# Compressed attention of a hybrid decoder layer: the softmax transposed per head pair to 96 rows, and its product with the values as one fp32r matmul of 512 columns

## The chip, the cores and the metric

The kernel runs on one core of a Trainium2 chip. The metric is the device time of one execution in microseconds; lower is better. A core has five engines that run side by side, each with its own in-order instruction queue: TensorE (PE in the rows; its weight loads are PEld), VectorE (DVE), ScalarE (ACT), GpSimd (POOL), and SyncE (SP), which here issues the transfers. TensorE writes into PSUM, a small memory of eight banks of 128 partitions by 512 float32 values; ScalarE and VectorE carry results from there to SBUF, the working memory.

## The reference

Two layers run one after the other on 256 tokens of width 1024. Each computes three attention branches from the same normalised input and merges them. The change touches one part of the first branch, the compressed attention: 256 tokens are compressed to 15 blocks for each of 2 key groups, and the 8 query heads (4 for each group) attend to the blocks of their group.

```python
def block(args):                       # one block of 128 queries
    qb, i = args
    t = i * Q_BLOCK + jnp.arange(Q_BLOCK)
    s = jnp.einsum('bqgrd,bngd->bgrqn', qb, k_c) * scale        # n: 15 compressed blocks
    p_c = _masked_softmax(s, cmp_end[None, :] <= t[:, None])
    o_c = jnp.einsum('bgrqn,bngd->bqgrd', p_c.astype(v_c.dtype), v_c)
...
o = g[..., 0, :] * to_bthd(o_c) + g[..., 1, :] * to_bthd(o_s) + g[..., 2, :] * to_bthd(o_w)
```

The other two terms, the selected blocks and the sliding window, and the two other branches are unchanged, as are the projections around them.

## The kernel before

Almost all the work is matrix products with weights that are streamed from HBM in chunks of 256 rows by up to 512 columns (`load_w`). A product of full accuracy is made of three products in the one-pass type fp32r: ScalarE rounds each chunk to a high half `whi` (line 161), VectorE forms the remainder `wlo` (line 162), and `gemm_steps` (line 263) adds high by high, low by high and high by low into the banks `mm`. The chunks are split two ahead of their use (`LEAD`), with three buffers for each half. `silu_path_T` (line 824) is the same with the operands' roles exchanged.

The attention is cut into units that are woven into these products. Each call of `tick` lets the unit in front compute its scores (`scores`), the one before it transpose its softmax (`transpose`), and the one before that multiply it with the values (`product`). The small matmuls of these steps stand in a list, `small`, and `hand_out` spreads them over the next chunk's matmuls, each tied behind one of them with `issue_after`. Within such ties the framework orders each engine's instructions itself, by a simulated timeline (`schedule_with_timeline_sim=True`), so the order in a trace is not that of the program.

The compressed attention is the class `Cmp`: one unit for each block of 128 queries and each layer, so four in all. In each layer the unit of the first block comes before the window units of the second block, and that of the second block before the forgetting branch. `Cmp.softmax` leaves in `e` (tile `ce`) 128 queries by 8 heads by 16 columns, the 15 probabilities and a zero. `Cmp.transpose` turns all of it in one 128 by 128 transposition (`put_T`, line 217) into a bank `T`, and `evac` copies it to `eT`, in turns on ScalarE (line 338) and VectorE (line 340). `Cmp.product` (line 979) multiplies it, in plain float32, with `Vc`: four products of 128 columns, one for each pair of heads, into the one bank `O`; a plain float32 product appears as two matmuls in the trace. Then `done_c` (lines 991 to 994) adds the result to the other two terms and splits it for the branch's projection.

`value` makes `Vc` once a layer: a product of the compressed hidden rows with `w2` (line 900) and one VectorE instruction (line 901) that writes the 128 by 512 block matrix with the mask `bmask`. `split_evac` (lines 371 and 373) is the usual way out of a transposition for the other units: a rounded copy by ScalarE into `PTh`, then the remainder by VectorE into `PTl`, two buffers each.

Of the kernel before, what the change touches and what calls it, by code (L numbers as in the profile page):

```python
# [31 lines left out]
def shape_constants():  # L32
    half = 32
    inv = (10000.0 ** (-np.arange(half, dtype=np.float32) / np.float32(half))).astype(np.float32)
    ang = np.arange(T, dtype=np.float32)[:, None] * inv[None, :]
    cos, sin = np.cos(ang).astype(np.float32), np.sin(ang).astype(np.float32)
    cos2 = np.concatenate([cos, cos], 1).reshape(NT, 128, 64).transpose(1, 0, 2)
    sin2 = np.concatenate([-sin, sin], 1).reshape(NT, 128, 64).transpose(1, 0, 2)
    ident = np.eye(128, dtype=np.float32)
    p = np.arange(128)  # L40
    ntri = -(p[:, None] <= p[None, :]).astype(np.float32)
    even = (p[:, None] == 2 * np.arange(64)[None, :]).astype(np.float32)
    odd = (p[:, None] == 2 * np.arange(64)[None, :] + 1).astype(np.float32)
    t = np.arange(T).reshape(NT, 128).T
    n = np.arange(15)
    cmask = np.where(16 * n[None, None, :] + 31 <= t[:, :, None], 0.0, NEG).astype(np.float32)

    bmask = 0.5 * (p[:, None] // 16 == np.arange(8)[None, :]).astype(np.float32)
    cm = np.where(p[None, :] <= p[:, None], 0.0, NEG).astype(np.float32)
    parts = [ident, cos2, sin2, ntri, even, odd, cmask, bmask, cm]  # L50
    cst = np.concatenate([a.reshape(128, -1) for a in parts], 1).astype(np.float32)
    return np.ascontiguousarray(cst)
# [7 lines left out]
def hybrid_kernel(ctx: ExitStack, tc, I, cst_d, out_d):  # L60
# [249 lines left out]
    def take(n):  # L310
        off[0] += n
        return cst[:, off[0] - n:off[0]]
# [4 lines left out]
    ntri = take(128)  # L317
    sel = [take(64), take(64)]
    cmask = take(30).rearrange("p (t n) -> p t n", t=2)
    bmask = take(8)  # L320
    cm = take(128)
    mhalf = S([128, 16], "mhalf")
    nc.gpsimd.memset(mhalf, -0.5)
# [247 lines left out]
    for l in range(2):  # L571
# [266 lines left out]
            mark((nm, l))  # L838


        Vc = S([128, 512], "Vc").rearrange("p (r g d) -> p r g d", r=4, g=2)

        def compress_out(i, hp):
            ch = S([128, 128], "cmph")
            nc.scalar.activation(ch, hp[:, 0:128], AF.Copy)

            def s1():
                q = pT()
                nc.tensor.transpose(q[:, 0:128], ch, ident)
                hs = S([128, 30], "cmphs")  # L850
                for g in range(2):
                    nc.vector.tensor_reduce(hs[:, g * 15:g * 15 + 15],
                                            q[:, 0:128].rearrange("p (j g n) -> p g n j", j=4, g=2)[:, g, 0:15],
                                            axis=AXX, op=ALU.add)
                th = S([128, 30], "cmpth")
                nc.scalar.activation(th, hs, AF.Tanh, scale=0.5)

                def s2():
                    if i == 0:
                        sT = S([128, 30], "sT")  # L860
                        nc.vector.scalar_tensor_tensor(sT, th, 1.0, hs, op0=ALU.add, op1=ALU.mult)
                        later(1, lambda: key(sT))
                    else:
                        sT = S([128, 4, 2, 16], "sTv")
                        nc.gpsimd.memset(sT, 0.0)
                        nc.vector.scalar_tensor_tensor(hs, th, 1.0, hs, op0=ALU.add, op1=ALU.mult)
                        nc.vector.tensor_copy(sT[:, :, :, 0:15], heads(hs, 2)[:, None].to_broadcast([128, 4, 2, 15]))
                        later(1, lambda: value(sT))
                later(1, s2)

            def key(sT):
                kp = pT()
                nc.tensor.matmul(kp[0:30, 0:64], sT, w2[:, 0, :], start=True, stop=True)
                kk = S([30, 64], "ckk")
                nc.vector.tensor_scalar(kk, kp[0:30, 0:64], 0.5, None, op0=ALU.mult)
                sq, ss, r = SQ()[0:30, 0:64], S([30, 1], "css"), S([30, 1], "cr")
                nc.scalar.activation(sq, kk, AF.Square, accum_out=ss)
                nc.gpsimd.tensor_scalar(r, ss, 1.0 / 64, EPS, op0=ALU.mult, op1=ALU.add)
                nc.gpsimd.tensor_tensor(r, r, mhalf[0:30, 0:1], op=ALU.pow)

                def s4():
                    kn = S([128, 128], "cmph")[0:30].rearrange("p (g d) -> p g d", g=2)
                    for g in range(2):
                        nc.vector.scalar_tensor_tensor(kn[:, g, :], kk, r, g4[0:30, 1, :], op0=ALU.mult, op1=ALU.mult)

                    def s5():
                        q2 = pT()
                        nc.tensor.transpose(q2[:, 0:30], kn.rearrange("p g d -> p (g d)"), ident[0:30, 0:30])
                        nc.scalar.activation(kcT[0][:, :, 0:15], heads(q2[:, 0:30], 2), AF.Copy)
                        for g in range(2):  # L890
                            gs = slice(g * 64, (g + 1) * 64)
                            nc.vector.tensor_tensor(kcT[1][gs, g, 0:15], q2[gs, g * 15:g * 15 + 15],
                                                    kcT[0][gs, g, 0:15].bitcast(F32), op=ALU.subtract)
                        mark(("kc", l))
                    later(1, s5)
                later(1, s4)

            def value(sT):
                vp = pT()
                nc.tensor.matmul(vp[:, 0:64], sT.rearrange("p r g n -> p (r g n)"), w2[:, 1, :], start=True, stop=True)  # L900
                nc.vector.tensor_tensor(Vc.rearrange("p r g d -> p (r g) d"), vp[:, 0:64][:, None, :].to_broadcast([128, 8, 64]), b3(bmask, 8, 64),
                                        op=ALU.mult)
                mark(("vc", l))
            later(1, s1)

# [19 lines left out]
        class Cmp:  # L925
# [40 lines left out]

            def transpose(self):
                def out(q):
                    self.eT = S([128, 128], "eT")
                    evac(self.eT, q[:, 0:128])  # L970
                put_T([lambda: self.e.rearrange("p h n -> p (h n)")], out)

            def product(self):
                box = []

                def one(r):
                    if not box:
                        box.append(pO())
                    nc.tensor.matmul(box[0][:, r * 128:(r + 1) * 128], Vc[:, r].rearrange("p g d -> p (g d)"), self.eT,  # L979
                                     start=True, stop=True)  # L980
                for r in range(4):
                    put(lambda r=r: one(r), *([lambda: self.done(box[0])] if r == 3 else []))

        oa_ = act_pair(4, "oT")

# [272 lines left out]
```

## Time and profile before

| | us |
|---|---|
| median of 3 runs | 637.11 (636.88 to 637.46) |
| the profiled execution | 637.58 |
| its span | 635.9 |

The profile is of one execution, of which the span covers all but 1.7 us. It gives busy time of each engine, waits and what ended them, the chain of work that ended last, and every instruction in order of time. A matmul's shown duration contains the time that it spends in the pipeline: matmuls that follow each other overlap, so what one costs TensorE is read from the distance of starts, or from the chain, where pieces do not overlap.

### The profile page before, as it was taken

Reading aid. Unit: us, or ns where it says so; the run is one execution under the profiler, and the core shown is the slowest. Engines: PE = TensorE matmul, PEld = TensorE weight load, DVE = VectorE, ACT = ScalarE, POOL = GpSimd, SP = SyncE. Lnnn points to the kernel's source line nnn. Section 1 sums busy time; section 2 is a strip of 40 time slices with the busy share of each in tenths; the row PEclk is TensorE's granted clock in tenths of the full one; section 3 lists DMA queues with packets and bytes.
Section 4 is the critical chain, followed back from the end, with each engine's and each line's share of the span. In section 5 each row is a group of like instructions: output and inputs, shape, how many; then the busy total and the mean of one; then the engine's idle time right before and its main releaser. Section 6 shows DMA issues by size and latency. Waiting matters only on the chain.

```text
span 635.9 us, 10280 instructions
## 1 busy us (share of the span) xinstructions
PE 623.9 (98%) x3567; PEld 532.2 (84%) x3567; DVE 472.7 (74%) x841; ACT 381.7 (60%) x810; POOL 175.5 (28%) x234
## 2 busy tenths in 40 slices
PE   7999999999999999999999999999999999999997
PEld 5699997788998888888887989977889888888885
DVE  3678897668977976956576799965799678777563
ACT  5766667455756676544476666855476666664441
POOL 1813403343413220704012233140053051042130
PEclk8999999999999999999999999999999999999999
DMA  8759775375345454546754695544644365445442
GB/s 298 170 159 282 230 173 161 101 207 169 104 130 139 132 161 133 164 138 195 234 178 109 195 336 159 150 140 133 172 122 140 99 172 160 137 128 166 166 149 82
DMA packets 75412, 104.51 MB, mean 164 GB/s; under 512 B 16832, under 2 KB 31456, under 8 KB 75360
## 3 DMA queue, kind: packets, MB, share of 16 engines
q1 hardware_dynamic: 75296, 103.84, 55.6%
q8 instruction: 28, 0.46, 0.3%
q14 instruction: 24, 0.20, 0.1%
q10 hardware_dynamic: 64, 0.02, 0.0%
HBM read 102.78 MB, written 1.05 MB: 163 GB/s over the span
## 4 chain that ended last, share of the span: by engine, by line
PE 94%; ACT 2%; DMA 1%; DVE 1%; issue 1%; SPq 0%; ACTq 0%
PE mm L263 60%; PE mm L824 11%; PE S L263 6%; PE T L217 6%; PE O L482 4%; PE S L1011 2%; DMA wraw<-in_w_mem_kv_dram 1%; PE S L1110 1%; PE S L918 1%; PE S L1170 1%; PE S L1108 1%; PE O L979 1%; ACT whi L161 1%; PE S L938 1%; ACT sq L363 0%
## 5 line engine op out<-in xcount | busy, mean ns | idle before, releaser
L162 DVE TENSOR_TENSOR wlo<-wraw,whi 128x1024 fp32r<-128x1024 f32 (+3 forms) x177 | 220.5, 1249 | 95.3 <-ACT whi L161 93.1
L161 ACT ACTIVATE whi<-wraw 128x1024 fp32r<-128x1024 f32 (+3 forms) x177 | 183.8, 1039 | 113.0 <-PE mm L263 71.4
L263 PE MATMUL mm<-whi,aTl 128*128 128x512 f32 (+1 forms) x480 | 189.2, 394 | 0.7 <-DVE aTl L396 0.6
L263 PE MATMUL mm<-whi,aTh 128*128 128x512 f32 (+1 forms) x480 | 188.0, 397 | 1.2 <-ACT whi L161 1.1
L263 PE MATMUL mm<-wlo,aTh 128*128 128x512 f32 (+1 forms) x480 | 184.7, 395 | 1.0 <-DVE wlo L162 1.0
L537 POOL TENSOR_TENSOR P<-P,d 128x512 f32<-128x512 f32 (+1 forms) x64 | 61.2, 971 | 208.0 <-DVE d L533 99.3
L263 PEld LDWEIGHTS mm<-whi,aTh 128*128 128x128 f32 x480 | 90.1, 189 | 19.6 <-ACT whi L161 2.3
L263 PEld LDWEIGHTS mm<-wlo,aTh 128*128 128x128 f32 x480 | 90.6, 189 | 18.3 <-DVE wlo L162 1.9
L263 PEld LDWEIGHTS mm<-whi,aTl 128*128 128x128 f32 x480 | 90.6, 189 | 17.4 <-DVE aTl L396 1.5
L824 PE MATMUL mm<-aTh,wlo 128*128 128x256 f32 x192 | 54.9, 288 | 0.0
L824 PE MATMUL mm<-aTl,whi 128*128 128x256 f32 x192 | 54.8, 286 | 0.0
L824 PE MATMUL mm<-aTh,whi 128*128 128x256 f32 x192 | 54.6, 285 | 0.0
L526 ACT ACTIVATE P<-S,m 128x256 f32<-128x256 f32 (+1 forms) x112 | 46.7, 427 | 7.6 <-DVE m L523 6.5
L1084 POOL TENSOR_TENSOR big<-big,t 128x512 f32<-128x512 f32 x16 | 28.2, 1776 | 58.9 <-DVE t L1083 53.9
L371 ACT ACTIVATE PTh<-T 128x512 fp32r<-128x512 f32 (+1 forms) x48 | 26.9, 560 | 25.7 <-PE T L217 25.4
L263 PE MATMUL mm<-whi,oTh 128*128 128x512 f32 x96 | 38.5, 404 | 0.6 <-ACT PTh L371 0.6
L263 PE MATMUL mm<-wlo,oTh 128*128 128x512 f32 x96 | 38.8, 407 | 0.0
L263 PE MATMUL mm<-whi,oTl 128*128 128x512 f32 x96 | 38.7, 403 | 0.0
L824 PEld LDWEIGHTS mm<-aTh,wlo 128*128 128x128 f32 x192 | 36.6, 191 | 0.4
L824 PEld LDWEIGHTS mm<-aTh,whi 128*128 128x128 f32 x192 | 36.6, 191 | 0.3
L824 PEld LDWEIGHTS mm<-aTl,whi 128*128 128x128 f32 x192 | 36.6, 191 | 0.2
L523 DVE TENSOR_REDUCE m<-S 128x2 f32<-128x512 f32 (+3 forms) x64 | 32.3, 515 | 2.7 <-PE S L1170 2.5
(229 smaller groups left out, 1002.9 us busy)
## 6 DMA issues: line engine op xcount, KB each, us to landing
wraw<-in_w_in_dram SPq DMA_DIRECT2D x112, 512.0 KB, 3.8
wraw<-in_w_out_dram SPq DMA_DIRECT2D x16, 512.0 KB, 4.1
wraw<-in_w_mem_kv_dram SPq DMA_DIRECT2D x15, 512.0 KB, 4.4
wraw<-in_w_branch_a_dram SPq DMA_DIRECT2D x16, 256.0 KB, 4.0
wraw<-in_w_branch_b_dram SPq DMA_DIRECT2D x8, 512.0 KB, 3.6
wraw<-in_w_branch_m_dram SPq DMA_DIRECT2D x8, 512.0 KB, 3.6
wraw<-in_w_in_dram SPq DMA_DIRECT2D x8, 408.0 KB, 3.6
wraw<-in_w_in_dram SPq DMA_DIRECT2D x8, 384.0 KB, 3.5
```

The lines of the kernel that those rows point to most:

```text
L161: nc.scalar.activation(wh[:, j, :n], v[:, j, :n], AF.Copy)
L162: nc.vector.tensor_tensor(wl[:, j, :n], v[:, j, :n], wh[:, j, :n].bitcast(F32), op=ALU.subtract)
L217: nc.tensor.transpose(q[0][0:b.shape[1], i * 128:(i + 1) * 128], b, ident)
L263: mi = nc.tensor.matmul(o_, a[:, kg, ts], w_[:, k, :n], start=(kg == 0 and i == 0), stop=(last and k == 1 and i == 2))
L371: nc.scalar.activation(hi, src, AF.Copy, scale=scale)
L482: nc.tensor.matmul(self.O[0:lhsT.shape[1], cols], lhsT, rhs, start=first, stop=False, skip_group_check=True)
L523: nc.vector.tensor_reduce(m[:, n:n + c], heads(sp[:, o_:o_ + w * c], c), axis=AXX, op=ALU.max, negate=True)
L526: nc.scalar.activation(self.P[:, k], sp[:, k], AF.Exp, bias=m[:, n:n + 1], accum_out=d[:, n:n + 1])
L537: nc.gpsimd.tensor_tensor(P3, P3, b3(d[:, n:n + c], c, w), op=ALU.mult)
L824: mi = nc.tensor.matmul(o_, w_, a[:, kg, :], start=(kg == 0 and j % 2 == 0 and i == 0), stop=(kg == 7 and i == 2), skip_group_check=True)
L1011: put(lambda j=j, k_=k_: nc.tensor.matmul(sp()[:, j * 256:(j + 1) * 256], QA[:, g, r0 + j, ts], k_, start=(j == 0 and k_ is kh), stop=(j = ...
L1084: nc.gpsimd.tensor_tensor(uv, uv, tn, op=ALU.add)
```

## The change

`Cmp.transpose` makes four transpositions instead of one, each of two heads (32 columns of `e`), into the same 32 partitions of one bank, side by side: 32 by 512. Three instructions carry it out of PSUM: a rounded copy (high part) to partitions 0 to 31, the remainder (low part) to 32 to 63, and the rounded copy again to 64 to 95. They write a tile of 96 by 512 that takes its buffers from those of `PTh`. `value` makes, in place of `Vc`, the tile `V3` of 96 by 128: the values' high part against the first two groups of rows and their low part against the third, so that `Cmp.product` is one fp32r matmul of 96 rows and 512 columns. The mask `bmask` shrinks from 8 to 2 columns, `sTv` from four copies to three.

```diff
-        Vc = S([128, 512], "Vc").rearrange("p (r g d) -> p r g d", r=4, g=2)
+        V3 = S([128, 128], "V3", dt=F32R)[0:96]
...
-                        sT = S([128, 4, 2, 16], "sTv")
+                        sT = S([128, 3, 2, 16], "sTv")
...
-                nc.tensor.matmul(vp[:, 0:64], sT.rearrange("p r g n -> p (r g n)"), w2[:, 1, :], start=True, stop=True)
-                nc.vector.tensor_tensor(Vc.rearrange("p r g d -> p (r g) d"), vp[:, 0:64][:, None, :].to_broadcast([128, 8, 64]), b3(bmask, 8, 64),
+                nc.tensor.matmul(vp[0:96, 0:64], sT.rearrange("p r g n -> p (r g n)"), w2[:, 1, :], start=True, stop=True)
+                vf = S([128, 128], "cmph")[0:96]
+                nc.vector.tensor_tensor(heads(vf, 2), vp[0:96, 0:64][:, None, :].to_broadcast([96, 2, 64]), b3(bmask[0:96], 2, 64),
                                         op=ALU.mult)
+                nc.scalar.activation(V3, vf, AF.Copy)
+                nc.vector.tensor_tensor(V3[64:96], vf[64:96], V3[64:96].bitcast(F32), op=ALU.subtract)
...
             def transpose(self):
                 def out(q):
-                    self.eT = S([128, 128], "eT")
-                    evac(self.eT, q[:, 0:128])
-                put_T([lambda: self.e.rearrange("p h n -> p (h n)")], out)
+                    self.eT = eT = S([128, 512], "PTh", bufs=2, dt=F32R)[0:96]
+                    nc.scalar.activation(eT[0:32], q[0:32], AF.Copy)
+                    nc.vector.tensor_tensor(eT[32:64], q[0:32], eT[0:32].bitcast(F32), op=ALU.subtract)
+                    nc.scalar.activation(eT[64:96], q[0:32], AF.Copy)
+                e = self.e.rearrange("p h n -> p (h n)")
+                put_T([lambda r=r: e[:, r * 32:(r + 1) * 32] for r in range(4)], out)
 
             def product(self):
-                box = []
-
-                def one(r):
-                    if not box:
-                        box.append(pO())
-                    nc.tensor.matmul(box[0][:, r * 128:(r + 1) * 128], Vc[:, r].rearrange("p g d -> p (g d)"), self.eT,
-                                     start=True, stop=True)
-                for r in range(4):
-                    put(lambda r=r: one(r), *([lambda: self.done(box[0])] if r == 3 else []))
+                def one():
+                    O = pO()
+                    nc.tensor.matmul(O, V3, self.eT, start=True, stop=True)
+                    self.done(O)
+                put(one)
```

## Rows read from the trace of the kernel before

**Rows 1.** The page of the profile: its parts 1 (busy time and share of the span, with the number of instructions) and 2 (tenths of busy time in 40 slices, and the granted clock of TensorE in tenths).

```profile
span 635.9 us, 10280 instructions
...
PE 623.9 (98%) x3567; PEld 532.2 (84%) x3567; DVE 472.7 (74%) x841; ACT 381.7 (60%) x810; POOL 175.5 (28%) x234
...
PEclk8999999999999999999999999999999999999999
```

**Rows 2.** The waits of TensorE over the whole span: who it waited for, us in total, times, longest.

```profile
PE T L217 <- DMA big<-in_mem_dram: 2.6, 1, 2.6
...
PE mm L263 <- ACT whi L161: 1.1, 3, 0.6
PE mm L263 <- DVE wlo L162: 1.0, 2, 0.5
```

**Rows 3.** The chain of waits in order of time from 150 to 165 us, around the first compressed unit of the first layer (start, us, what).

```profile
154.89 0.55 PE T L217 x5
...
156.39 1.39 PE mm L263 x6
157.77 0.89 PE O L979 x8
158.66 0.44 PE T L217 x4
```

**Rows 4.** The same view from 186 to 193 us, around the second compressed unit of the first layer.

```profile
187.41 0.11 PE T L217
187.51 0.59 PE mm L824 x5
...
191.76 0.89 PE O L979 x8
```

**Rows 5.** The same view around the two compressed units of the second layer (460 to 470 and 495 to 503 us).

```profile
467.29 0.89 PE O L979 x8
...
501.27 0.89 PE O L979 x8
```

**Rows 6.** The same view from 78 to 80 us and from 135 to 143 us: float32 products with a stationary side of 64 columns (L720) and the product that makes the compressed values (L900).

```profile
78.84 0.62 PE T L720 x16
...
136.17 0.17 PE T L900 x2
```

**Rows 7.** TensorE's instructions in order of time, 213.6 to 213.8 us (start, us, line, operands: moving and then stationary side, then the size of the stationary and of the moving side): products with moving sides of 128 columns.

```profile
213.61 0.22 PE L482 MATMUL O<-PTh,fV 128*128 128x128 f32 x1
213.67 0.22 PE L482 MATMUL O<-PTl,fV 128*64 128x128 f32 x1
213.73 0.43 PE L1108 MATMUL S<-aTl,aTh 65*128 65x128 f32 x2
```

**Rows 8.** Groups of instructions by line, with shapes kept apart (count, then busy us, mean ns of one, idle before): copies out of PSUM and the differences beside them.

```profile
L338 ACT ACTIVATE eT<-T x2: 277/277/277, 155.0 to 464.5; 128x128 f32<-128x128 f32 x2
...
L373 DVE TENSOR_TENSOR PTl<-T,PTh 128x512 fp32r<-128x512 f32 x32 | 21.8, 681 | 1.1 <-ACT PTh L371 1.1
...
L371 ACT ACTIVATE PTh<-T 128x512 fp32r<-128x512 f32 x32 | 19.0, 595 | 18.9 <-PE T L217 18.8
...
L554 ACT ACTIVATE tm<-O 64x512 f32<-64x512 f32 x8 | 4.7, 591 | 2.2 <-PE O L482 2.1
...
L901 DVE TENSOR_TENSOR Vc<-T,cst 128x512 f32<-128x512 f32 x2 | 1.4, 692 | 0.1
```

**Rows 9.** Readers of one PSUM tile on two engines: ScalarE and VectorE in order of time (lines 661 to 663), and who waited for line 794.

```profile
81.92 0.27 ACT L661 ACTIVATE KH<-T 64x128 fp32r<-64x128 f32 x1 [0.39 <-DVE KL L663]
...
81.62 0.27 DVE L663 TENSOR_TENSOR KL<-T,KH 64x128 fp32r<-64x128 f32 x1
...
  ACT big L793: 3.8, 2
```

**Rows 10.** ScalarE in order of time after the transposition of the first compressed unit.

```profile
155.04 0.28 ACT L338 ACTIVATE eT<-T 128x128 f32<-128x128 f32 x1
155.47 0.60 ACT L371 ACTIVATE PTh<-T 128x512 fp32r<-128x512 f32 x1 [0.16 <-PE T L217]
```

**Rows 11.** VectorE in order of time in the same place.

```profile
155.62 0.68 DVE L366 TENSOR_REDUCE ss<-sq 128x8 f32<-128x512 f32 x1
...
157.52 0.69 DVE L1048 TENSOR_TENSOR t<-mm,rf 128x512 f32<-128x512 f32 x1 [0.29 <-POOL rf L352]
...
163.38 3.19 DVE L162 TENSOR_TENSOR wlo<-wraw,whi 128x1024 fp32r<-128x1024 f32 x2
```

**Rows 12.** VectorE in order of time around the second compressed unit of the first layer.

```profile
187.55 0.29 DVE L340 COPY eT<-T 128x128 f32<-128x128 f32 x1 [1.49 <-PE T L217]
...
192.69 0.69 DVE L991 TENSOR_TENSOR o<-o,O 128x512 f32<-128x512 f32 x1 [1.97 <-PE O L979]
```

**Rows 13.** Busy time of the engines in stretches (us, then PE, PEld, DVE, ACT, POOL with their instructions, granted clock, DMA share, GB/s).

```profile
160.00:175.00 15.00, 15.00 (x102) 13.71 (x101) 14.85 (x28) 11.79 (x28) 5.42 (x4) 1.00 0.42 112
...
470.00:490.00 20.00, 20.00 (x145) 18.71 (x144) 19.57 (x38) 14.22 (x32) 7.83 (x6) 1.00 0.44 126
```

**Rows 14.** TensorE in order of time after the first compressed unit: a product of the window branch, and two products of a gemm.

```profile
163.33 0.28 PE L482 MATMUL O<-PTh,VN 128*128 128x256 f32 x1
...
166.56 0.39 PE L263 MATMUL mm<-whi,aTl 128*128 128x512 f32 x1
...
167.85 0.48 PE L263 MATMUL mm<-wlo,aTh 128*128 128x512 f32 x1
```

More of the change, by code (lines that the diff above doesn't have):

```diff
@@ L46, in shape_constants @@
     cmask = np.where(16 * n[None, None, :] + 31 <= t[:, :, None], 0.0, NEG).astype(np.float32)
-    bmask = 0.5 * (p[:, None] // 16 == np.arange(8)[None, :]).astype(np.float32)
+    bmask = 0.5 * ((p[:, None] // 16) % 2 == np.arange(2)[None, :]).astype(np.float32)
     cm = np.where(p[None, :] <= p[:, None], 0.0, NEG).astype(np.float32)
@@ L319, in hybrid_kernel @@
     cmask = take(30).rearrange("p (t n) -> p t n", t=2)
-    bmask = take(8)
+    bmask = take(2)
     cm = take(128)
@@ L863, in s2 @@
                     else:
-                        sT = S([128, 4, 2, 16], "sTv")
+                        sT = S([128, 3, 2, 16], "sTv")
                         nc.gpsimd.memset(sT, 0.0)
                         nc.vector.scalar_tensor_tensor(hs, th, 1.0, hs, op0=ALU.add, op1=ALU.mult)
-                        nc.vector.tensor_copy(sT[:, :, :, 0:15], heads(hs, 2)[:, None].to_broadcast([128, 4, 2, 15]))
+                        nc.vector.tensor_copy(sT[:, :, :, 0:15], heads(hs, 2)[:, None].to_broadcast([128, 3, 2, 15]))
                         later(1, lambda: value(sT))
```

## Prediction

> **What bounds the kernel now.** I read the page first: TensorE is busy 623.9 of 635.9 us, VectorE 74% and ScalarE 60%, and the granted clock is at its upper level (2.4 GHz) in every slice but the first [rows 1]. A busy TensorE can still hide stalls, so the second view is its waits: the longest is 2.6 us at the start of the kernel, for a transfer; for the high and low halves of the weights, which the two other engines make, it waits 1.1 and 1.0 us in the whole span [rows 2]. So time that is taken out of TensorE's queue is taken out of the kernel, unless a new wait eats it. Third, the chain of waits around the compressed units, four in all: it stays on TensorE from piece to piece, and there each piece has its own, not overlapping, time [rows 3 to 5].
>
> **What the product costs now, and then.** The eight matmuls of a compressed product take 0.89 us, the same in all four units [rows 3 to 5], or 0.11 each. Their moving side has only 128 columns. Six fp32r matmuls of 512 columns take 1.39 [rows 3], or 0.23 each, and two fp32r matmuls that move 128 columns with a stationary side of 64 and then 128 start 0.06 apart [rows 7]. So the short ones are not limited by the 128 columns that they move, but by the 128 that they load. The new product moves 512 columns once and its load hides behind the matmul before it: 0.23. No row has a matmul of 96 rows; the nearest, with 128, move the same columns, so I take 0.23 at both ends. Saved: 0.89 - 0.23 = 0.66 us a unit.
>
> **What the transpositions cost.** A lone transposition costs 0.11 [rows 4], a group of four 0.44 [rows 3]: again 0.11 for each 128 columns loaded. The change makes four that load 32 columns and move 128 (the identity). No row shows that shape. Upper bound: the load of 32 costs as much as that of 128, or the four are scattered, each in front of a matmul that loads 128; then 0.44. Lower bound: sixteen small products that load 64 and move 64 columns take 0.62 [rows 6], 0.039 each; three of these and 0.11 for the last, behind which a full load has to follow, are 0.23. Between: three that move 128 columns at 0.06 [rows 7], and 0.11, make 0.29. I take this, since the step of 0.06 comes from the row with the same moving side and a short load. Against today's 0.11 the transpositions add 0.18 (0.12 to 0.33).
>
> The Trainium skill has a rule for this ("TensorE: Matmul & The Clock Gate", section "LDWEIGHTS (loading the stationary operand)"): a load takes its number of columns divided by 1.2, in ns, whatever the number of rows. For 128 columns that is 107 ns, which the 0.11 of rows 3 bears out; for 64 it would be 53 ns, more than the 0.039 us of rows 6. By the rule, with the 56 ns that the same page gives for 128 moving columns, a group would be an estimated 0.275 us, and the four units together would save 0.06 us more than by my rows.
>
> **The sum on TensorE.** A unit gains 0.66 - 0.18 = 0.48 us (0.33 to 0.54); four units 1.92 (1.3 to 2.2). The product of `value`, two matmuls at 0.17 once a layer [rows 6], loads 96 columns in place of 128: a quarter of at most 0.11 for one load that isn't hidden, 0.03 in each layer, so 0.03 for both as a middle between 0 and 0.06. Together -1.95 us. On the profiled execution (span 635.9, its own time 637.58) that gives 635.6. The median of the runs shown is 0.47 below that execution; on it the sum gives **635.2**, with 634.8 to 635.8 from the bounds.
>
> **What is added on the two other engines.** In place of one copy of 128x128 (0.28 on ScalarE in the first units, 0.29 on VectorE in the second [rows 8, 12]) there are two ScalarE copies and one VectorE difference of 32x512. A copy of 64x512 takes 591 ns and one of 128x512 595 [rows 8], so the number of partitions doesn't matter, and I take 0.60 and 0.68 for 32 too. ScalarE gets 0.92 us more in a first unit and 1.20 in a second; VectorE 0.68 and 0.39. In `value`, VectorE's 692 ns [rows 8] give way to 96x128 and 32x128, by the nearest rows about 0.29 and 0.27 [rows 9, 12]; ScalarE gets 0.28. It is done long before the product, and I cost it at nothing.
>
> I cost the rest at nothing too: what hides it is TensorE's other work, the gemm's chunks that are split two ahead. If that cover were gone, VectorE's additions would be worth 2 x 0.68 + 2 x 0.39 = 2.1 us, and ScalarE's 4.2. VectorE is the engine to look at: it is busy 14.85 of 15 us right after the first unit, and 19.57 of 20 at the same place of the second layer [rows 13]. The gap before L1048 there is 0.29 us [rows 11], so 0.4 of the new 0.68 pushes its whole queue back, up to the two weight halves at 163.38 [rows 11]. Around the second units it idles for 1.49 and 1.97 us [rows 12].
>
> **The added wait.** Before, one instruction carried `eT` out. Now there are three that read one bank, and the rows say how such readers go: in lines 661 to 663 ScalarE begins its next copy only when VectorE has ended its read of the same tile (81.62 + 0.27, then 81.92), and L793 has waited 3.8 us for L794 [rows 9]. So the second copy, though it needs nothing from the difference, waits for it: 0.60 + 0.68 + 0.60 = 1.88 us in a row. The Trainium skill names a reason ("PSUM — Partial Sum Buffer", section "Terms"): two engines on one bank and the same partitions at once are an error, so that they must be kept apart; the trace agrees, as rows 9 show. Behind the waiting copy stand, in ScalarE's queue, the rounded copy at 155.47 [rows 10] and the exponentials that follow it. Their users come late: the product that reads that copy starts at 163.33 [rows 14].
>
> Does TensorE wait for the chain? The first copy can start at 155.04 [rows 10], and the product stood at 157.77 [rows 3]: 2.7 us. Four transpositions end 0.18 later, which leaves some 2.5 for 1.88, and 0.6 for what stands in the way: L366 in VectorE's queue (0.68 from 155.62, [rows 11]) and the other copy on ScalarE (0.60 [rows 10]). Tight, but the order isn't fixed: after 166.56 TensorE went on past a weight half that came late, and took it up at 167.85 [rows 14]. For the second units there are 4.2 us (187.51 to 191.76 [rows 4]). The buffers don't add a wait: `eT` joins the two of `PTh`, the unit before has been multiplied by then, and the next unit to need its buffer has the product in front of it already.
>
> **The rivals.**
> - *Half of it is given back in the first units.* If the chain meets L366 and the copy at 155.47, it is about 0.7 over; or VectorE's push of 0.4 reaches the weight halves. At 0.4 to 0.7 in each of the two first units, 0.8 to 1.4 of the 1.95 are lost: 636.0 to 636.6 on the median, 636.3 in the middle. For it: rows 11 and 13. Against it: TensorE itself runs 0.48 earlier, and it found other work at 166.56.
> - *The small transpositions are not cheaper.* At the upper bound of 0.44 a group the gain is 4 x 0.33 = 1.3: 635.8. For it: no row shows 32 columns, and `hand_out` may scatter them. Against it: rows 6.
> - *The product stands and waits.* This one ends slower. TensorE's queue is in order; if the product keeps its place while its operand comes through two busy queues, with a pair of weight halves like that of rows 11 (3.19 us) ahead of the difference, beside which only the first copy's 0.60 runs, the chain becomes 1.88 + 3.19 - 0.60 = 4.5, 2.0 over the 2.5 there are. Two first units then cost 4.0, and the sum is +2.05: 639.2. It decides the sign by over 0.2% from a chain of some 4.1 us. Against it: no weight half stands between 155 and 157.5 in rows 10 and 11.
>
> **How the numbers follow.** Forecast 0.58, half given back 0.20, transpositions not cheaper 0.11, product waits 0.11. The likeliest is the forecast: 635.2. A measurement tells about 0.2% from no change, 1.27 us here; below 635.84 is faster. The forecast lies there but for its edge, the second rival by half; the first is within 0.2%. That makes faster 0.60, same 0.29, slower 0.11. The range runs from 634.5 (the lower bounds, and 0.3 for the reordering of other work) to 636.8 (the first rival's end with 0.2 on top); it leaves the third rival out and some of each edge.
>
> **What the next profile would show.** Right: in the chain, one L-product of 0.23 in place of 0.89 in each unit, groups of four transpositions near 0.29, TensorE busy about 2 us less and its waits as short as before. The first rival: TensorE idle before L482, L263 or the new product, ended by VectorE, some 0.5 each at 155 to 170 and 465 to 480. The second: groups of 0.44. The third: idle of over 1.5 us before the new product, ended by ScalarE. What would make me wrong altogether: a 96-row matmul of 512 columns that takes two passes, or a new order that leaves waits elsewhere.

## The result, and the profile after

The change makes the kernel slower: 645.21 us (median of 6 runs, 642.16 to 645.78) against 637.32 of the kernel before (6 runs, 636.88 to 638.2), a ratio of 1.0116 [1.0105, 1.0128]. The forecast was 635.2, its range 634.5 to 636.8. The profiled execution took 645.2, 7.6 more than that of before.

The page of the kernel after, for [rows 1]:

```profile
span 643.5 us, 10246 instructions
...
PE 627.4 (97%) x3551; PEld 533.6 (83%) x3551; DVE 474.2 (74%) x845; ACT 385.8 (60%) x818; POOL 176.3 (27%) x234
...
PEclk9999999999998999999999999999999899999999
```

The span is 7.6 us longer. TensorE is busy 3.5 us more, though it has less to do, and idle 4.1 us more (643.5 - 627.4 = 16.1, before 635.9 - 623.9 = 12.0). The line of the granted clock has two new 8s, and its first slice is no 8 any more. So two things are to be found: idle time, and time at a lower clock.

What the prediction had costed comes first: the chain of waits around the first compressed unit, for [rows 3].

```profile
154.77 0.88 PE T L217 x8
...
155.89 0.47 PE S L1014 x4
...
159.36 0.23 PE O L983
159.60 0.44 PE T L217 x4
```

The product costs 0.23, as forecast. The transpositions don't cost 0.29: eight of them, the unit's four of 32 columns and a window unit's four of 128, take 0.88, which is 0.11 each and 0.44 for the four. TensorE's queue shows the two groups starting at 154.61 and 155.05. Their weight loads did become shorter (the loads of `ce` in the kernel before and then in this one: how many, then the least, median and most ns):

```profile
L217 PEld LDWEIGHTS T<-cst,ce x4: 137/138/141, 154.5 to 496.6; 128*128 128x128 f32 x4
...
L217 PEld LDWEIGHTS T<-cst,ce x16: 94/95/96, 154.4 to 502.7; 128*32 128x32 f32 x16
```

The three instructions out of PSUM in the same place, on ScalarE and then on VectorE, in order of time, for [rows 10, 11]:

```profile
155.25 0.59 ACT L974 ACTIVATE PTh<-T 32x512 fp32r<-32x512 f32 x1 [0.44 <-PE T L217]
...
157.24 0.59 ACT L976 ACTIVATE PTh<-T 32x512 fp32r<-32x512 f32 x1
```

```profile
156.22 0.68 DVE L975 TENSOR_TENSOR PTh<-T,PTh 32x512 fp32r<-32x512 f32 x1
...
159.58 0.69 DVE L1051 TENSOR_TENSOR t<-mm,rf 128x512 f32<-128x512 f32 x1 [0.36 <-POOL rf L352]
160.18 0.15 DVE L533 TENSOR_TENSOR d<-d,gat 128x2 f32<-128x2 f32 x1
```

The three come one after the other, as forecast (155.25, 156.22, 157.24), and the product, at 159.36, doesn't wait for them; it has moved 1.6 back, behind other work (before, 157.77). Around this unit TensorE doesn't wait at all, as the prediction said. But two lines lower VectorE's queue stands in a new order: L1051 (before: L1048), which waits for GpSimd, is ahead of L533; before, L533 came first, at 158.78. This small step of a window unit is 1.40 us later, and GpSimd's work on that unit (L537) starts at 160.50, before at 159.61.

TensorE's waits over the whole span, for [rows 2]:

```profile
PE S L1111 <- ACT P L526: 4.7, 2, 2.3
```

This line is new: 4.7 us, in two waits, one in each layer. Most of the others stand in the first 32 us, where nothing was changed. Here is the place in the first layer, before and after. First the kernel before, TensorE and then VectorE in order of time:

```profile
193.88 1.03 PE L1110 MATMUL S<-aTl,aTh 65*128 65x256 f32 x4
194.88 0.50 PE L263 MATMUL mm<-whi,aTh 128*128 128x512 f32 x1
```

```profile
193.41 0.69 DVE L993 SCALAR_TENSOR_TENSOR o<-o,sg 128x512 f32<-128x512 f32 x1
194.14 0.69 DVE L808 SCALAR_TENSOR_TENSOR sg<-sq,mm 128x512 f32<-128x512 f32 x1
```

Then the kernel after, TensorE and VectorE:

```profile
193.61 0.49 PE L983 MATMUL O<-PTh,V 96*128 96x512 f32 x1
196.44 0.49 PE L1111 MATMUL S<-aTl,aTh 65*128 65x128 f32 x2 [2.34 <-ACT P L526]
...
197.34 0.50 PE L263 MATMUL mm<-whi,aTh 128*128 128x512 f32 x1
...
197.99 0.63 PE L263 MATMUL mm<-wlo,aTh 128*128 128x512 f32 x1
198.42 0.63 PE L263 MATMUL mm<-whi,aTh 128*128 128x512 f32 x1
...
201.31 0.39 PE L263 MATMUL mm<-whi,aTl 128*128 128x512 f32 x1
201.54 0.40 PE L263 MATMUL mm<-wlo,aTh 128*128 128x512 f32 x1
```

```profile
194.27 0.29 DVE L523 TENSOR_REDUCE m<-S 128x1 f32<-128x128 f32 x1
194.48 0.68 DVE L994 TENSOR_TENSOR o<-o,O 128x512 f32<-128x512 f32 x1
195.08 0.62 DVE L523 TENSOR_REDUCE m<-S 128x1 f32<-128x128 f32 x2
195.61 0.68 DVE L996 SCALAR_TENSOR_TENSOR o<-o,sg 128x512 f32<-128x512 f32 x1
...
196.61 0.67 DVE L808 SCALAR_TENSOR_TENSOR sg<-sq,mm 128x512 f32<-128x512 f32 x1
```

Line 808 is the last step of a SiLU gate: it writes a buffer of `sg`, and it is the last reader of one of the three banks `mm`. Lines 993 (before) and 996 (after) close the second compressed unit, and are the last readers of the buffer of `sg` that this L808 is to write. In the kernel before, L993 starts at 193.41, L808 at 194.14, and the gemm at L263 goes on at 194.88, without idle time but right behind it: the slack is zero. In the kernel after, the product is at 193.61 (before 191.60), L994 at 194.48, L996 at 195.61 and L808 at 196.61. TensorE stands 2.34 us behind the product. Between the closing steps stand row maxima of the next units (L523), so VectorE's queue makes the step longer still. Two things come back to TensorE late: at 196.44 a bank `S` for the next scores, given back by the exponentials (L526), which had waited for VectorE's row maxima behind L994; and at 197.34 the bank `mm`, given back by L808, with which the gemm goes on. The profile names the first, since it came first; that the second is the one to look at is shown only by the experiments below.

And look at the distance of the starts after the stall. From 197.99 on they are 0.43 apart, where 0.23 is the rule; from 201.31 they are 0.23 again. That is the granted clock. The stretches table shows it in both layers (columns as in [rows 13]):

```profile
198.00:201.40 3.40, 3.40 (x11) 2.80 (x10) 2.22 (x7) 0.61 (x1) 0.97 (x2) 0.53 0.00 0
508.00:510.00 2.00, 1.36 (x4) 1.16 (x5) 2.00 (x5) 2.00 (x8) 0.97 (x2) 0.60 0.00 0
510.00:517.00 7.00, 7.00 (x26) 5.67 (x24) 3.62 (x8) 2.22 (x4) 0.97 (x2) 0.63 0.00 0
```

A clock of 0.53 for 3.4 us loses 1.6, 0.60 for 2 us 0.8, and 0.63 for 7 us 2.6: 5 us, an estimate from these three lines. With it the 7.6 is nearly accounted for. Busy: about +5 for the clock, -1.3 for the work that the change saves (four units of 0.33, see below), together near the measured +3.5. Idle: +4.7 for the two stalls, and what is left to the measured +4.1, -0.6, for all other waits together.

### The profile page after: what moved, and what is told of

The parts are those of the page before. It is cut to its first block, busy times and chain, and to the rows that moved or that the text cites. A ratio compares the mean times of both kernels' runs of the same rounds, so it can differ in the third digit from the quotient of the medians.

```text
span 643.5 us, 10246 instructions
## 1 busy us (share of the span) xinstructions
PE 627.4 (97%) x3551; PEld 533.6 (83%) x3551; DVE 474.2 (74%) x845; ACT 385.8 (60%) x818; POOL 176.3 (27%) x234
## 4 chain that ended last, share of the span: by engine, by line
PE 94%; DVE 2%; ACT 2%; DMA 1%; issue 0%; SPq 0%; ACTq 0%; DVEq 0%
PE mm L263 61%; PE mm L824 11%; PE T L217 6%; PE S L263 6%; PE O L482 4%; PE S L1014 2%; DMA wraw<-in_w_mem_kv_dram 1%; PE S L1113 1%; PE S L922 1%; PE S L1173 1%; DVE wlo L162 1%; PE S L1111 1%; ACT whi L161 1%; ACT sq L363 1%; PE S L942 0%; DVE S L517 0%
## 5 line engine op out<-in xcount | busy, mean ns | idle before, releaser
L263 PE MATMUL mm<-whi,aTl 128*128 128x512 f32 (+1 forms) x480 | 190.7, 397 | 0.8 <-DVE aTl L396 0.6
L263 PE MATMUL mm<-whi,aTh 128*128 128x512 f32 (+1 forms) x480 | 188.6, 399 | 1.8 <-ACT aTh L395 1.2
L263 PE MATMUL mm<-wlo,aTh 128*128 128x512 f32 (+1 forms) x480 | 184.9, 396 | 1.1 <-DVE wlo L162 1.1
L537 POOL TENSOR_TENSOR P<-P,d 128x512 f32<-128x512 f32 (+1 forms) x64 | 59.9, 949 | 203.2 <-DVE d L533 102.8
L263 PEld LDWEIGHTS mm<-whi,aTh 128*128 128x128 f32 x480 | 91.1, 190 | 19.8 <-ACT aTh L395 1.6
L263 PEld LDWEIGHTS mm<-wlo,aTh 128*128 128x128 f32 x480 | 91.1, 190 | 19.0 <-DVE wlo L162 1.9
L263 PEld LDWEIGHTS mm<-whi,aTl 128*128 128x128 f32 x480 | 91.2, 190 | 18.1 <-DVE aTl L396 1.4
L526 ACT ACTIVATE P<-S,m 128x256 f32<-128x256 f32 (+1 forms) x112 | 47.0, 430 | 13.3 <-DVE m L523 12.2
L371 ACT ACTIVATE PTh<-T 128x512 fp32r<-128x512 f32 (+1 forms) x48 | 26.9, 559 | 26.9 <-PE T L217 24.6
L263 PE MATMUL mm<-whi,oTh 128*128 128x512 f32 x96 | 38.8, 404 | 0.4 <-DVE t L1137 0.4
L263 PE MATMUL mm<-whi,oTl 128*128 128x512 f32 x96 | 38.6, 402 | 0.0
L263 PE MATMUL mm<-wlo,oTh 128*128 128x512 f32 x96 | 38.5, 406 | 0.0
L373 DVE TENSOR_TENSOR PTl<-T,PTh 128x512 fp32r<-128x512 f32 (+1 forms) x48 | 30.7, 640 | 5.7 <-ACT PTh L371 5.4
```

Source lines behind the costliest of these rows:

```text
L263: mi = nc.tensor.matmul(o_, a[:, kg, ts], w_[:, k, :n], start=(kg == 0 and i == 0), stop=(last and k == 1 and i == 2))
L371: nc.scalar.activation(hi, src, AF.Copy, scale=scale)
L373: nc.vector.tensor_tensor(lo, src, hi.bitcast(F32), op=ALU.subtract)
L526: nc.scalar.activation(self.P[:, k], sp[:, k], AF.Exp, bias=m[:, n:n + 1], accum_out=d[:, n:n + 1])
L537: nc.gpsimd.tensor_tensor(P3, P3, b3(d[:, n:n + c], c, w), op=ALU.mult)
```

## The experiments

Theory 1: TensorE starves at the end of the second compressed unit of each layer, through a ring of buffers. `sg` has two buffers for the three gates SA, SB and SM. The gate of SM takes SA's buffer, and SA's last reader is the second compressed unit's closing step. So a later end of this unit holds L808; L808 holds a bank of `mm`; and the bank holds the second half of the next gemm, the memory branch's query projection. In the kernel after, a fall of the clock follows each stall. The rivals look where the prediction had looked: the serial way out itself, with ScalarE's second copy held behind VectorE; the work added to VectorE and ScalarE; the price of the product or of the transpositions. Each expectation says what its theories give. In the code shown, `...` stands for lines left out.

**The gate's buffer freed.** SM's gate gets the buffer of a tile that is idle at that time (`Lc`), in the kernel after (e1) and in that of before (e2):

```diff
...
-            sg = S([128, 4, T], "sg", bufs=2)
+            sg = S([128, 4, T], "Lc") if nm == "SM" else S([128, 4, T], "sg", bufs=2)
...
```

> The changed kernel, with one thing more: the third SiLU gate of a layer (SM) is written to the buffer of Lc, which is idle by then, and no longer waits for the first gate's buffer, whose last reader is the end of the second compressed unit (L996). Theory 1 (starvation): TensorE ran dry at 193.8 to 196.4 us and at the same place of layer 2 because the gate's VectorE step (L808), and behind it the bank that the next gemm half needs, stood behind the compressed unit's end; the two stalls of 2.3 us and the fall of the clock to 1.2 GHz after them (3.4 and 6.8 us at half speed, worth 5.1) make the whole loss. Then both stalls and both clock falls are gone here, and the time is that of before less TensorE's own gain: four units at 0.89 - 0.23 - 0.33 = 0.33 us (the four transpositions take 0.44 in the trace of after), 1.3 together: 636.0, 635.0 to 637.0. Theory 2 (the three-part way out of PSUM costs it, with ScalarE held behind VectorE): nothing of that is removed here, so the time stays within 1.5 us of after, 644 to 646.

> The kernel before, with the same edit alone (the third gate in the buffer of Lc). It tells whether e1 differs from before by the change or by this edit. In the trace of before the gate's step ended at 194.83 and the gemm half that needs its bank began at 194.88, without idle time of TensorE. Theory 1: no stall to remove, 636.8 to 637.8, so e1 is 1 to 1.6 us below this one. Theory 2: the same here, and e1 some 7 us above it.

Measured: e1 634.77 (634.46 to 635.0), 0.9957 [0.9942, 0.9972] of before; e2 636.65 (636.19 to 637.07), 0.9985 [0.9975, 0.9995]. Both came out just below what theory 1 had said (635.0 to 637.0 and 636.8 to 637.8). One buffer is worth 10.4 us to the kernel after (645.21 to 634.77) and 0.9 to that of before (637.55 in the runs beside it), where a wait for `PTh` (L371) of 0.3 a layer is gone. VectorE in e1, and the stretches that contain the old stalls:

```profile
184.93 0.69 DVE L808 SCALAR_TENSOR_TENSOR Lc<-sq,mm 128x512 f32<-128x512 f32 x1 [0.34 <-ACT sq L807]
...
201.64 0.68 DVE L996 SCALAR_TENSOR_TENSOR o<-o,sg 128x512 f32<-128x512 f32 x1
```

```profile
130.00:205.00 75.00, 74.97 (x444) 65.68 (x442) 59.95 (x114) 49.20 (x109) 25.18 (x39) 1.00 0.52 149
440.00:515.00 75.00, 74.98 (x444) 65.58 (x443) 60.06 (x114) 48.92 (x108) 19.79 (x21) 1.00 0.51 145
```

L808 starts at 184.93, nearly 12 us earlier, and no longer behind the unit's close, which is as late as 201.64 and holds nothing up. TensorE is busy 74.97 of 75 us at full clock. The whole loss of the kernel after is behind this ring. Between the two freed kernels the change is worth -1.88 us, so in this order of the queues it does save time; e7, below, is another order, and there it doesn't.

**One unit only.** e3 changes the first unit of each layer, e4 the second (`self.t == 1` in place of 0). Both make `Vc` and `V3`, which costs VectorE one step more a layer:

```diff
...
+                if self.t == 0:
+                    put_T([lambda r=r: e[:, r * 32:(r + 1) * 32] for r in range(4)], out3)
+                else:
+                    put_T([lambda: e], out)
...
```

> Only the first compressed unit of each layer is changed (four transpositions, three-part way out, one product of 512 columns); the second is as before. Both Vc and V3 are made, one VectorE step more a layer, and the old eT takes the buffer of cmph. Theory 1, in the form that the first unit's added work in the stretch where VectorE is full pushes the window units back by some 2 us, and with them the second unit's end: the stall of over 1.5 us before the third forgetting unit's scores is there in both layers though the second unit is untouched: 642 to 646. Theory 2 in the form that the second unit's own longer way out is what came too late: no stall, 636 to 637.5.

> Only the second compressed unit of each layer is changed; the first is as before. Both Vc and V3 are made, and the old eT takes the buffer of cmph. Theory 1 with the first unit as the cause: the window units end as in before, the second unit's product comes some 1 us later than before at most, no stall over 0.5 us, no fall of the clock: 636 to 638. Theory 2 in the form that the second unit's own longer way out came too late: stalls of some 2 us and the clock's fall as in after: 642 to 646.

Measured: e3 640.33 (638.74 to 641.13), 1.0037 [1.0026, 1.0049]; e4 637.15 (636.83 to 637.75), 0.9995 [0.9985, 1.0004]. TensorE's wait in each (lines of these two kernels stand one or two lower, L810 is L808):

```profile
PE S L1134 <- ACT P L528: 2.6, 2, 1.3
```

```profile
PE mm L264 <- DVE sg L810: 1.4, 2, 0.7
```

In e3 the gate's last step starts at 196.75 and in e4 at 194.66. So the stall is at the end of the second unit, but what makes this end late is mainly the change of the first, 40 us earlier; the second unit's own longer way out gives 0.7 a layer. The sizes missed: e3 was expected at 642 or more, with stalls over 1.5, and e4 with none over 0.5. The two don't add up to the kernel after either (+2.8 and -0.4 against the runs beside them, together far from +7.9).

**The added work alone.** The kernel before, with three instructions like the new ones into a buffer of `PTh` that nobody reads:

```diff
...
+                    nc.scalar.activation(xT[0:32], q4, AF.Copy)
+                    nc.vector.tensor_tensor(xT[32:64], q4, xT[0:32].bitcast(F32), op=ALU.subtract)
+                    nc.scalar.activation(xT[64:96], q4, AF.Copy)
```

> The kernel before, plus, in each compressed unit, the changed kernel's three instructions out of PSUM (a ScalarE copy, a VectorE difference, a ScalarE copy, each 32x512, from the same bank, into a buffer of PTh); nothing reads their result, and TensorE's instructions are those of before. If the added work on the two engines is what pushes the second unit's end back (theory 1), TensorE gets a stall in front of the second half of the MQ gemm or of the third forgetting unit's scores in both layers, 0.7 to 2.5 us each, ended by VectorE's gate step or ScalarE's exponentials, with or without a fall of the clock: 638.5 to 643. If the push comes from the new transpositions and product in TensorE's list (rival), there is no stall, and the time is that of before: 637 to 638.

Measured: 642.25 (640.23 to 643.81), 1.0071 [1.0048, 1.0093].

```profile
PE mm L263 <- DVE sg L808: 3.9, 2, 2.0
```

Nothing was changed in TensorE's work, and most of the loss is there (4.7 us), at the same place and with the ring's own name on it.

**The ring filled by another cause.** To see that lateness alone does it, two plain VectorE copies of 128x512 go ahead of the second unit's close in the kernel before (e9), and the same with the gate's buffer freed (e10):

```diff
+                if t:
+                    for _ in range(2):
+                        nc.vector.tensor_copy(S([128, 512], "tm", bufs=2), O)
```

> The kernel before, with two added VectorE copies of 128x512 in front of the second compressed unit's closing steps in each layer (done_c; nothing reads the copies). TensorE's and ScalarE's work and the first units are those of before; the only thing that is moved is the end of the second unit, by 2 x 0.68 = 1.4 us. Theory 1: the gate's step L808 moves from 194.1 to about 195.5, TensorE has nothing else and waits for it 0.7 to 1.5 us in each layer: 638.5 to 640.5 without a fall of the clock, up to 643 with one in each layer. Rival (the loss comes from work in the first unit's stretch, where VectorE is full, and not from this end): at most 0.5 us, 637.5 to 638.

> The same two added copies, with the third gate in the buffer of Lc as in e1 and e2. Theory 1: nothing hangs on the end of the second unit any more, so the copies cost nothing: within 0.7 us of e2 (636.65), no stall ended by L808. Rival: the copies cost here what they cost in e9.

Measured: e9 641.73 (639.93 to 642.83), 1.0063 [1.0043, 1.0082]; e10 636.4 (635.75 to 636.62), 0.9979 [0.997, 0.9989]. VectorE and then TensorE in e9:

```profile
192.68 1.29 DVE L993 COPY tm<-O 128x512 f32<-128x512 f32 x2 [1.97 <-PE O L979]
193.89 0.68 DVE L994 TENSOR_TENSOR o<-o,O 128x512 f32<-128x512 f32 x1
...
194.84 0.68 DVE L996 SCALAR_TENSOR_TENSOR o<-o,sg 128x512 f32<-128x512 f32 x1
...
195.97 0.68 DVE L808 SCALAR_TENSOR_TENSOR sg<-sq,mm 128x512 f32<-128x512 f32 x1
```

```profile
193.87 1.03 PE L1113 MATMUL S<-aTl,aTh 65*128 65x256 f32 x4
196.71 0.50 PE L263 MATMUL mm<-whi,aTh 128*128 128x512 f32 x1 [1.81 <-DVE sg L808]
...
198.72 0.63 PE L263 MATMUL mm<-whi,aTl 128*128 128x512 f32 x1
```

The close is pushed from 193.41 to 194.84, L808 starts 1.83 later than before, and TensorE stands 1.81: nothing is absorbed, as a slack of zero says. The clock then falls (0.43 apart at 198.72). With the buffer freed the same copies cost nothing (636.4 against 636.65 of e2), and TensorE is never idle in this stretch:

```profile
130.00:205.00 75.00, 75.00 (x447) 66.19 (x446) 61.27 (x112) 47.01 (x105) 24.36 (x38) 1.00 0.52 150
```

**The serial way out undone.** In the kernel after, both ScalarE copies go first, and the difference after them, so that ScalarE isn't held behind VectorE (e6); the same with the freed buffer (e7):

```diff
+                    nc.scalar.activation(eT[64:96], q[0:32], AF.Copy)
                     nc.vector.tensor_tensor(eT[32:64], q[0:32], eT[0:32].bitcast(F32), op=ALU.subtract)
-                    nc.scalar.activation(eT[64:96], q[0:32], AF.Copy)
```

> The changed kernel with the three instructions out of PSUM in another order: both ScalarE copies, then VectorE's difference, so that no ScalarE instruction waits for VectorE. The work is the same. Theory 2 (ScalarE held behind VectorE is the loss): near 635.5 to 636.5, without stalls. Theory 1 (what counts is when the second unit ends, since the gate's buffer hangs on it): the first units' added VectorE work is still there, so the second unit still ends later than in before, and some 0.5 to 1.5 us of stall a layer stay, without a fall of the clock if they are short: 637 to 640.

> The order of e6 and the third gate in the buffer of Lc as in e1. Theory 1: with the gate free the end of the second unit doesn't matter, so this is as fast as e1 within 0.7 us: 634.1 to 635.5, no stall of TensorE over 0.6 us between 130 and 620 us. Theory 2: the order of the copies is worth at least 1 us beside e1: under 633.8.

Measured: e6 644.1 (643.08 to 645.99), 1.0105 [1.0086, 1.0124], against 1.0116 of the kernel after; e7 638.22 (637.73 to 638.84), 1.0011 [1.0002, 1.002]. In e6:

```profile
PE mm L263 <- DVE sg L808: 5.6, 2, 2.8
```

The rival falls: with ScalarE released from the wait, the loss stays. But both expectations missed. In e6 the stall is as long as ever, 2.8 a layer. e7 has lost the stall, but is 3.45 above e1. Its span is 3.0 longer, 1.4 of it busy time and 1.6 idle; three new waits are seen:

```profile
PE S L1111 <- ACT P L526: 0.7, 2, 0.4
PE mm L263 <- ACT oTh L371: 0.7, 2, 0.3
PE mm L263 <- DVE oTl L373: 0.4, 2, 0.2
```

The last two stand at 253.6 and 563.5, in front of the forgetting branch's projection, some 50 us behind the second units. These waits are about the 1.6 of idle time; the order of the instructions differs in many places, and the rest stays open. e7 is also 1.6 above e2, the freed kernel without the change, so a new order alone can cost more than the change saves.

**Less work.** The kernel after without the low parts: one ScalarE copy, a product of 32 rows. It leaves out the low parts' contribution.

```diff
...
-                    nc.vector.tensor_tensor(eT[32:64], q[0:32], eT[0:32].bitcast(F32), op=ALU.subtract)
-                    nc.scalar.activation(eT[64:96], q[0:32], AF.Copy)
...
-                    nc.tensor.matmul(O, V3, self.eT, start=True, stop=True)
+                    nc.tensor.matmul(O, V3[0:32], self.eT[0:32], start=True, stop=True)
...
```

> The changed kernel without the low parts: one ScalarE copy carries the transposed softmax out, and the product has 32 rows (high part by high part alone, so the low parts' contribution is left out). The gate's buffer is as in after. Theory 1: VectorE has less to do than in before, the second unit ends no later than in before but for TensorE's order, and TensorE's own gain of 1.3 us shows: 634.5 to 637. If the four transpositions or the single product alone upset the list, the stall of about 2 us a layer is still there: 641 to 645.

Measured: 639.52 (639.35 to 641.3), 1.0035 [1.0021, 1.0049].

```profile
PE mm L263 <- DVE sg L808: 3.6, 2, 1.8
```

With one copy for each unit, as before (but of 32x512, 0.59 in place of 0.28), GpSimd's L537 is at 160.63, near its place in the kernel after, and the stall comes, 1.8 us a layer. So the difference on VectorE and the second copy are not needed for it, and theory 1's 634.5 to 637, which rested on VectorE having less to do, missed; the time is between the two that were expected. Its five runs fall in two groups, 639.35 to 639.52 at a mean clock of 1.0 and 641.0 to 641.3 at 0.993 to 0.995: one fall of the clock is worth about 1.7 us here.

**A control.** The kernel before with the engines that copy `eT` swapped (`evq = [1]`):

> A control: the kernel before with the two engines of evac in the other order, so that the first unit's eT is copied by VectorE (0.29 us) and the second's by ScalarE (0.28). If the order that the framework lays is upset by any touch of the first unit, VectorE's gate step d (L533, 158.78 in before) falls behind the multiplication that waits for GpSimd's rf, the window units come 1 to 2 us later, and the stalls of theory 1 appear: 639 to 643. If it takes an addition of the size of the change's, the order and the time stay those of before: 636.8 to 638.

Measured: 637.31 (636.81 to 637.71), 0.9995 [0.9986, 1.0005]. Not any disturbance of this place turns the order. The control leaves one thing open: it adds no work, but it takes no buffer of `PTh` for the first unit either, and all kernels whose order turned (after and e1, e3, e5 to e8) do both. No run takes the buffer without the longer copies, or the copies without the buffer.

All in one table. The start of the gate's last step and the stall are of the first layer, in the profiled execution:

| | us | gate's last step starts | TensorE's stall |
|---|---|---|---|
| before | 637.32 | 194.14 | 0 |
| after | 645.21 | 196.61 | 2.34 |
| e3, first unit | 640.33 | 196.75 | 1.3 |
| e4, second unit | 637.15 | 194.66 | 0.7 |
| e5, added work | 642.25 | 196.33 | 2.0 |
| e6, copies first | 644.1 | 195.74 | 2.8 |
| e8, high part | 639.52 | 195.95 | 1.8 |
| e9, late end | 641.73 | 195.97 | 1.8 |
| e11, swapped | 637.31 | 193.72 | 0 |
| e1, after, freed | 634.77 | 184.93 | 0 |
| e2, before, freed | 636.65 | 185.94 | 0 |
| e10, late end, freed | 636.4 | 186.24 | 0 |
| e7, copies first, freed | 638.22 | 184.73 | 0 |

In the rows that are not freed a start before 194.2 costs nothing and one after it stalls TensorE; a freed buffer takes the step out of the chain. How long the stall is depends also on when TensorE's other work runs out, which differs with the order.

## Why the prediction was wrong

- *What the product costs now, and then.* Right: 0.89 to 0.23 in each unit. The 96 rows took one pass.
- *What the transpositions cost.* Wrong in size: 0.44, the upper bound, not 0.29. The step that failed here is "not limited by the 128 columns that they move, but by the 128 that they load". The change made the load shorter, 95 ns in place of 138, and the matmul stayed as it was. What the rows leave is the moving side. In the chain after, two float32 matmuls of 256 columns take 0.45 (L1113 at 192.91, 0.22 each), four fp32r ones of 256 columns 0.47 (L1014 at 155.89, 0.12 each), all with a load of 128. So a float32 column costs about twice an fp32r one, and a transposition moves 128 float32 columns whatever it loads. The step of 0.06 [rows 7] was of the other type; and the matmul at 213.73 there loads 128 columns and yet starts 0.06 behind the one before it. The estimate of 0.275 by the Trainium skill ("TensorE: Matmul & The Clock Gate", section "LDWEIGHTS (loading the stationary operand)") falls as well: a group with 32 columns loaded cost 0.44, no less than one with 128.
- *The sum on TensorE.* With 0.44 a unit gains 0.33, four 1.3, the second rival's number. The freed kernels' profiled executions differ by 1.4 (636.36 and 635.00), their medians by 1.88. This is near the 1.3; where the rest of the 1.88 lies is not shown.
- *What is added on the two other engines.* The durations were right (588, 680 and 586 ns, 1.85 together). In the first unit they took 2.58 from end to end, since the difference stood behind L366 and the second copy behind exponentials, about what the prediction had allowed for. That "VectorE is the engine to look at" was right as well.
- *The added wait.* Right that the product would not stand: no matmul waited for `eT`, and the weight load in front of the product 0.5 us in two units together. ScalarE wasn't idle in front of the second copy (L976) in any of the four units of the kernel after, and e6, which takes that wait away, loses as much.
- *The step that failed:* "I cost the rest at nothing too: what hides it is TensorE's other work". It holds where TensorE has other work. The prediction asked only whether TensorE would wait for the new operand, and looked some ten us ahead of it. It did not follow the unit's result to its last reader and ask what buffer that reader gives back. The trace of before had the answer: L993, L808, L263 at 193.41, 194.14, 194.88, with no slack at all. The price of losing that cover was put at 2.1 us of VectorE's time; it was 4.7 of stalls and about 5 of clock. This term, put at nothing, turned the sign: with the gate's buffer freed (e1) the change comes out at 634.77, inside the forecast's range, though 0.9 of that is what the freed buffer is worth by itself (e2).
- *The rivals.* None was this one. The first had the right engine, but the loss at 155 to 170; the third had the right sign, but a wait before the new product. The last sentence, "a new order that leaves waits elsewhere", is what happened, and had no chance of its own.

What the runs show: the ring (e1 against after, e9 against e10), the slack of zero (e9), and that it is mainly the first unit's change that makes the second late (e3, e4). The way from the first unit to the second is read from rows, and no run cuts it: VectorE's turned order at 159.58 and 160.18, GpSimd's L537 0.9 later there, the last L537 of the window units at 181.14 where it was at 179.00, and the second unit's transposition behind the last product of these units. TensorE before and after:

```profile
187.13 0.28 PE L482 MATMUL O<-PTl,VN 128*64 128x256 f32 x1
187.24 0.27 PE L217 MATMUL T<-cst,ce 128*128 128x128 f32 x1
```

```profile
190.15 0.28 PE L482 MATMUL O<-PTl,VN 128*64 128x256 f32 x1
190.26 0.60 PE L217 MATMUL T<-cst,ce 128*32 128x128 f32 x4
```

The second unit's own softmax is not late. VectorE's last step of it, before and after:

```profile
184.50 0.28 DVE L964 TENSOR_TENSOR ce<-ce,cd 128x128 f32<-128x128 f32 x1
```

```profile
182.94 0.29 DVE L968 TENSOR_TENSOR ce<-ce,cd 128x128 f32<-128x128 f32 x1
```

By these rows it is the window units in front of it that hold it up. e4 and e11, which don't turn the order, have the first L537 at 159.70 and 159.31 and this transposition at 187.32 and 186.61; e3, e5, e6 and e8, which do, have them at 160.5 to 161.1 and 189.5 to 190.9. Why the order turns, with three more instructions (e5) and with one longer copy (e8), but not in e11, is open, and so is whether the work does it or the buffer of `PTh`.

## What to carry to other kernels

When a step moves later, follow its result to the last reader, and ask which buffer that reader gives back and who is next in that ring; a ring of two shared by three tiles can tie units 40 us apart. A step that starts the moment it is released, with the bottleneck engine's next instruction right behind it, has no slack, and the profile shows no wait there until something is late: such places are to be listed before an edit is costed at nothing. And a stall of the matrix engine may be charged twice, once as idle time and once as lower clock behind it, so a kernel that loses such a stall should be tried again with the edit that seemed not to pay: e1, the change with one buffer freed, is faster than both kernels, by 0.4% against before. But the order that the framework lays has a price of its own (e7), so such a fix has to be measured too.

## What the runs showed of the hardware

- After the idle stretches of 2.3 us in the kernel after, TensorE began at full clock, fell to half of it (1.2 GHz) some 1.5 us later, and stayed there for 3.4 us in the first layer; in the second the clock was already low when it began again, and the low stretch lasted to about 515.3, 6.7 us. In e9 an idle stretch of 1.8 was followed by such a fall in the first layer, and the like one in the second layer was not. The 0.7 of e4 was not either. Not every execution of one kernel has the same falls: e9's runs go from 639.93 at a mean clock of 1.0 to 642.83.
- A float32 transposition that loads 32 columns costs TensorE 0.11 us, as one that loads 128 does, though its load is shorter (95 ns, 138). The sixteen products of [rows 6], at 0.039 with 64 columns each, fit neither rule exactly.
- A copy or difference of 32x512 takes 586 to 680 ns, as that of 128x512: a quarter of the partitions saves nothing.
